# Turning cached keys beside the even layer: each load, turn and store pinned to a projection unit

## The chip, the cores and the metric

The kernel runs on one core of one Trainium2 chip. The metric is the device time of one execution in microseconds (us), as the median over several runs. A core has a matrix engine (TensorE, PE), a vector engine (VectorE, DVE), a scalar engine (ScalarE, ACT), a general engine (GpSimd, POOL), and a queue engine (SyncE, SP) that issues almost all transfers here. Each engine works off its own row of instructions in the order in which they stand; an instruction that waits for something holds everything behind it on its engine.

## What is computed

One inference step of a decoder with two layers and width 1024, on a prompt of 2048 tokens together with 8 sequences that each decode 4 tokens on top of 2048 cached tokens. Layer 0 runs two groups of heads on one input projection: four heads of a gated linear recurrence (HGRN2) and four heads of forgetting attention. Layer 1 is a gated linear attention (GLA). The part that matters here is the forgetting attention of the decoding sequences, whose cached keys and values lie in pages of 128 tokens that a page table names:

```python
def fox_sample(q, k, v, log_f, k_pages, v_pages, logf_pages, page_table):
    ...
    k_past = k_pages[page_table].reshape(db, -1, H, dh)      # 8 sequences x 16 pages x 128 tokens, 4 heads of 128
    v_past = v_pages[page_table].reshape(db, -1, H, dh)
    ...
    logit_past = jnp.einsum('bthd,bshd->bhts', q, k_past) * scale + cum_new[..., None] + suffix_past[:, :, None, :]
    logit_new = jnp.einsum('bthd,bshd->bhts', q, k) * scale + cum_new[..., None] - cum_new[:, :, None, :]
    ...
    p = jax.nn.softmax(jnp.concatenate([logit_past, logit_new], axis=-1), axis=-1)
    return einsum(p[..., :P], v_past) + einsum(p[..., P:], v)

def even_mixer(h, w_in, ...):
    proj = h @ w_in                                          # one projection for both groups of heads
    qa, fa, ia, ga, qb, kb, vb, gb, fb = _split(proj, ...)
    o_a, s_a = gated_linear_chunked(qa, 1 - f, ia, log(f), s0)   # HGRN2
    ...                                                      # forgetting attention, gates, output projection
```

## The kernel before, in words

**Even layer.** `phase_even` (from L1122) works the prompt in two halves of 1024 tokens, and each half is 16 projection units: unit numbers 0 to 15 and 16 to 31. A unit multiplies the half's normalized activations with one block of weights, in a few chunks of columns. `staged` (L1266) runs the units one after another; beside each chunk it issues a step of a later unit's weight preparation (load of the raw weights, row maxima, powers and scales, split into two halves) and calls `beside`. Names of weights tell the unit: `w_Ag`, `w_A10f`/`Aqf`, `w_Bq`, `w_Bk`, `w_Bv`, `w_Cqk`; `pt_...`/`pf_...` are the products in PSUM, `Bk`, `Bv`, `Bg` their evicted results, `Bks`, `Bvs` and `kd`, `vd`, `qd`, `sgd` their split copies and the places in DRAM to which they are stored. `lin_attn` is the recurrence of HGRN2, in `dg`, `gd_A`, `gl_A`, `qA`, `fA`, `o_A`, `py_A`, `y_A`; it runs beside the units, its results go to `yT`. `pow_o` and `kc` are small scale calculations.

**Keys.** The cached keys make 32 tiles, each of four pages of one sequence. A tile `kp` (128 partitions x 4 x 512, 1 MB) comes by four transfers of 256 KB. The page numbers are first loaded to registers of SP (`page_regs`, L1520), and each transfer takes its address from one of them (`page_load`, L1528). For TensorE the keys must lie with the head's dimension on the partitions: DVE turns each of the four pages with one STREAM_TRANSPOSE (`turn_block`, L1532) into a tile `kT`. For the first `PRE` = 16 tiles this is done ahead, in the even layer, by `ahead` (L1534): the turned tile is stored to a place in DRAM (L1548, 1 MB), and the forgetting attention reads it back as `ktd` (L1592). The other 16 are loaded and turned in the forgetting attention itself.

`ahead` is called from `beside`, for chunks 1 and 3 of each unit, with x counting up by two per unit, and starts at x = `PRE0` = 32, the first unit of the second half. Only its page loads are held behind one another:

```python
            with ExitStack() as st:
                if n:
                    st.enter_context(self.tc.issue_after(self.last_page.ins))
                regs = self.page_regs(n % 2, n // 2)
            for x in range(4):
                self.last_page = self.page_load(t, "cache_fox_k", regs[x], x)
```

**What sets the order.** The kernel is written with a scheduling layer. It takes the recorded instructions, models their times, and puts each engine's instructions into a fixed order; work without dependences on its neighbours can come out far from the place in which it was written. `with self.tc.issue_after(x.ins)` pins what is recorded in it to stand behind instruction `x` on its engine's row. Tiles live in rings of buffers by tag: `kp` and `kT` share the ring "wr" with the raw weights (`EWR` buffers); a tile can be written only when the reader of the ring's previous holder is done. Before, the 16 tiles come out back to back: their loads are issued from 352.1 to 583.3 us of the span, their turns stand from 383.2 to 593.8.

**Forgetting attention.** `phase_fox` (from L1350) begins when the last unit's values are there. It interleaves the prompt's attention (scores `s`, DVE's masking and maximum in L1418, `L`, `mx`, `nm`, and the loads of each step: `q`, `k` by a transposing load, `v`, `cb`, `fsg`, L1380 to L1395) with the attention of the decoding sequences: `qs`, `kn`, `sgs`, `vn` (L1604) and `q` (L1617) are its small loads, `qz` its scaled queries (L1625), `sc` its scores against the turned keys (L1692).

Of the kernel before, what the change touches and what calls it, by code (L numbers as in the profile page):

```python
# [8 lines left out]
F32 = mybir.dt.float32  # L9
# [6 lines left out]
ALU = mybir.AluOpType  # L16
# [3 lines left out]
P = 128  # L20
D = 1024
KT = D // P
# [6 lines left out]
NH = 4  # L29
# [10 lines left out]
EWR = 3  # L40
# [10 lines left out]
PRE = 16  # L51
PRE0 = 32
PAST = 3
# [74 lines left out]
class Kern:  # L128
# [200 lines left out]
    def half_unit(self, pool, pps, w, cols, key, nm, undo=None, k=1.0, also=(), raw=("wr", WU), scaler=None, keep=None):  # L329
# [7 lines left out]
        def fetch():  # L337
            t["raw"] = pool.tile([P, KT, raw[1]], F32, tag=raw[0], name=f"wr_{nm}")
            for a, off, n, src in self.sources(w, cols, h):
                with nc.allow_non_contiguous_dma(reason="a few columns"):  # L340
                    nc.sync.dma_start(t["raw"][:, a * h : (a + 1) * h, off : off + n], src)

# [36 lines left out]
    def kept_unit(self, pool, kept, width, nm):  # L379

        t = {}

        def load():
            t["w"] = Parts(self.w_tile(pool, nm, width))
            self.nc.sync.dma_start(t["w"].both.rearrange("p x k c -> p (x k c)"), kept[:, : 2 * KT * width])

        return lambda: None, load, lambda: None, lambda: t["w"]
# [294 lines left out]
    def silu2(self, wp, dst, ps, n, nm, c):  # L682

        nc = self.nc
        th = wp.tile([P, 512], F32, tag="th", name=f"th_{nm}")
        nc.scalar.activation(dst, ps, AF.Copy, scale=c)  # L686
        self.last_th = nc.scalar.activation(th[:, :n], dst, AF.Tanh, scale=0.5)
        self.last_si = nc.vector.scalar_tensor_tensor(dst, th[:, :n], 1.0, dst, ALU.add, ALU.mult)


    def lin_attn(self, wp, pps, hf, h, dv, q, f, k, v, vs, sg, gain, S, s0, s_out, p_out, ydst, nm):
# [26 lines left out]
        def finish(po, g, rows, ncol, cnt):  # L718
# [9 lines left out]
            def out(c0, dcol):  # L728
                for t in range(nt):
                    py = pps.tile([P, 512], F32, tag="gr", name=f"py_{nm}{g}{t}")  # L730
                    for c in range(cnt):
                        nc.tensor.transpose(py[:, c * rows : (c + 1) * rows], on[:rows, c, t * P : (t + 1) * P],
                                            self.ident[:rows, :rows])
                    y = wp.tile([P, 512], F32, tag="y", name=f"y_{nm}{g}{t}")
                    w = TS if g == "S" else cnt * rows

                    for x in range(2 if g == "S" else 1):
                        yo, src, gate = y[:, :w], py[:, :w], sg[t][:, c0 : c0 + w]
                        if g == "S":
# [3 lines left out]
                        nc.vector.scalar_tensor_tensor(yo, src, gain[:, t : t + 1], gate, ALU.mult, ALU.mult)  # L743
                    nc.sync.dma_start(ydst[t][:, dcol : dcol + w], y[:, :w])

            return out

        def levels(ws):
            for w in ws:
# [186 lines left out]
    def even_half(self, hf, act, wpool, wp, pps, npool, S):  # L936
# [54 lines left out]
        def mk_qf(h):  # L991
            def run(W):
                nm = f"A{hf}{h}"
                if h not in self.scales2:
# [6 lines left out]
                                        ALU.mult, ALU.add)  # L1001
                nc.vector.tensor_scalar(f[h][:, :n], f[h][:, :n], self.fb[:, h : h + 1], self.fa[:, h : h + 1],
                                        ALU.mult, ALU.add)
# [5 lines left out]
        def store_cols(dst, t, c0, m):  # L1009

            for a, cnt, dc in self.pieces(hf):
                lo, hi = max(a, c0), min(a + cnt, c0 + m)
                if lo < hi:
                    nc.sync.dma_start(dst[:, dc + lo - a : dc + hi - a], t[:, lo - c0 : hi - c0])

        def mk_bq(hp, which):
            def run(W):
                if which == "q" and hf == 0:
                    self.fox_scale("q", hp)
                for j in range(2):  # L1020
                    h = 2 * hp + j

                    def ev(ps, c0, m, h=h):
                        t = wp.tile([P, 512], F32, tag="c2", name=f"B{which}{hf}{h}{c0}")
                        if which == "q":
                            up, few = self.fsc["q", hp][0], max(0, c0 + m - HALF)
                            u = t.bitcast(F16).rearrange("p (x t) -> p x t", x=2)[:, :, : m - few]
                            nc.scalar.activation(u[:, 0], ps[:, : m - few], AF.Copy, scale=up)
                            nc.vector.scalar_tensor_tensor(u[:, 1], ps[:, : m - few], up, u[:, 0], ALU.mult,
                                                           ALU.subtract)  # L1030
                            dc = hf * HALF + c0
                            nc.sync.dma_start(self.qd[h][:, :, dc : dc + m - few], u)
                            if few:
# [11 lines left out]
        def mk_bkv(hp, which):  # L1045
# [3 lines left out]
            def run(W):  # L1049
# [5 lines left out]
                def ev(ps, g, cnt, m):  # L1055
# [12 lines left out]
                    if m == P:  # L1068
                        u = held[1]
                        for j in range(cnt):  # L1070
                            src = ps[:, j, :256].rearrange("p (h d) -> p h d", h=2)
                            hi, lo = (u[:, g % 2 + j, :, x] for x in range(2))
                            nc.scalar.activation(hi, src, AF.Copy, scale=self.cu[which, hp])
                            nc.vector.scalar_tensor_tensor(lo, src, self.cu[which, hp], hi, ALU.mult, ALU.subtract)
                    if m < P:
# [4 lines left out]
                    elif (g + cnt) % 2 == 0:  # L1080
                        if which == "v":
# [5 lines left out]
                        dst = {"k": self.kd, "v": self.vd}[which][hf][g0 * P : (g0 + 2) * P, 2 * hp : 2 * hp + 2]  # L1087
                        self.last_row = nc.sync.dma_start(dst.rearrange("(g s) h x d -> s g (h x d)", s=P),
                                                          u.rearrange("p g h x d -> p g (h x d)"))
# [32 lines left out]
    def phase_even(self):  # L1122
# [4 lines left out]
        with pool("act", side="right") as ap, pool("w", side="right") as w0, pool("wl", side="right") as wp1, \  # L1127
                pool("wk") as wp0, pool("nrm") as n0, pool("stt") as sp, pool("ps", space=PSUM) as pp0:
            wpool = Pool(w0, {"w": 3, "wr": EWR, "rm": 2, "pow": 2, "lr": 2})
            wp = Pool(wp0, {"c4": 7, "sam": 1, "v4": 3, "sg": 3, "pd": 1, "kt": 2, "y": EY, "xpad": 1, "vs": 3,  # L1130
# [15 lines left out]
            def beside(x):  # L1146
                self.ahead(wpool, x)
                x -= 33
# [101 lines left out]
            drain(last)  # L1250
            self.ahead(wpool, 64)

# [13 lines left out]
    def staged(self, us, a, b, beside=None):  # L1266
# [15 lines left out]
        for j in range(a, b):  # L1282
# [250 lines left out]

    def ahead(self, pool, y):  # L1534


        y -= PRE0
        if y % 2:
            if y // 2 < PRE and y > 0:
                t, tag = self.key  # L1540
                self.key = pool.tile([P, NH * 4, P], F32, tag=tag, name=f"kT{y // 2}"), y // 2
                for x in range(4):
                    self.turn_block(self.key[0], t, x)
            return
        n = y // 2
        if 0 < n <= PRE:
            kt, m = self.key
            self.nc.sync.dma_start(self.kT[m], kt.rearrange("p a s -> p (a s)"))  # L1548
        if 0 <= n < PRE:
            tag = "lr" if y + PRE0 < 32 else "wr"  # L1550
            t = pool.tile([P, 4, 512], F32, tag=tag, name=f"kp{n}")
            with ExitStack() as st:
                if n:
                    st.enter_context(self.tc.issue_after(self.last_page.ins))
                regs = self.page_regs(n % 2, n // 2)
            for x in range(4):
                self.last_page = self.page_load(t, "cache_fox_k", regs[x], x)
            self.key = t, tag

# [724 lines left out]
```

## Time and profile before

| | |
|---|---|
| median of three runs | 2336.53 us (2333.63, 2340.0, 2336.53) |
| the profiled execution's own time | 2332.04 us |
| its span in the trace | 2330.4 us |
| mean granted TensorE clock | 0.987 |
| PE busy | 2203.2 us, 95% of the span |
| DVE busy | 1399.7 us, 60% |
| ACT / POOL busy | 992.1 us, 43% / 731.2 us, 31% |
| transfers | 395.48 MB, 170 GB/s on the mean |

The shares are over the whole span. A share of 95 for PE leaves 127 us of idle time, and in which stretches that lies is read from sums by stretch. The second half of the even layer runs from about 480 to 893 us of the span, the start of the forgetting attention follows. In the rows of the timeline a bracket at the end gives how long the engine sat idle ahead of this instruction, and what released it.

### The profile page before, as it was taken

What the parts mean: (1) busy time and instruction counts of PE and PEld (TensorE: products, weight loads), DVE (VectorE), ACT (ScalarE), POOL (GpSimd) and SP (SyncE); (2) the same over time, 40 slices, a digit from 0 to 9 for tenths busy, and PEclk for the clock granted to TensorE, in tenths of its full rate; (3) what the DMA queues carried; (4) which work ended last, traced back from release to release, by engine and by line L of the source; (5) the groups of instructions that cost most, each with busy time, mean ns of one, the idle gap of its engine ahead of it and who ended that gap; (6) DMA issues with size and microseconds to landing.
All of it is one profiled execution on the core that took longest, in us unless ns stands there. A gap on an engine that the chain in (4) does not pass through costs nothing.

```text
span 2330.4 us, 58046 instructions
## 1 busy us (share of the span) xinstructions
PE 2203.2 (95%) x23316; PEld 1572.3 (67%) x23316; DVE 1399.7 (60%) x3138; ACT 992.1 (43%) x2200; POOL 731.2 (31%) x788
## 2 busy tenths in 40 slices
PE   7999999897999998887998999999999999999998
PEld 5677677763565685554445888777677666666887
DVE  7756568635555456697677545366664655547554
ACT  6434354220221223444566543546544535545343
POOL 2223434000111113423345445144551432322232
PEclk9999999998999999999999999999999999999999
DMA  7343447999642239799884968523233531115554
GB/s 238 120 126 104 147 128 228 321 248 290 202 150 92 95 116 299 252 221 254 283 259 147 338 189 253 147 84 128 76 105 90 128 99 58 47 58 164 165 184 158
DMA packets 364144, 395.48 MB, mean 170 GB/s; under 512 B 108401, under 2 KB 303282, under 8 KB 355682
## 3 DMA queue, kind: packets, MB, share of 16 engines
q1 hardware_dynamic: 361730, 385.15, 55.0%
q0 software_dynamic: 2144, 6.62, 0.8%
q8 instruction: 183, 3.00, 0.5%
q14 instruction: 87, 0.71, 0.1%
HBM read 261.58 MB, written 113.20 MB: 161 GB/s over the span
## 4 chain that ended last, share of the span: by engine, by line
PE 43%; DVE 5%; DMA 5%; issue 2%; ACT 2%; POOL 2%; SPq 1%; POOLq 0%; DVEq 0%; ACTq 0%
PE pt_o L629 4%; PE pt_o L630 4%; PE pt_o L631 4%; PE pt_Cv L629 2%; PE pt_Cv L631 2%; PE pt_Cv L630 2%; DMA pgcache_fox_k<-in_cache_fox_k 2%; PE pt L1454 1%; PE o_C L913 1%; PE pv L1772 1%; DVE L L1418 1%; PE gl_C L760 1%; PE fo L629 1%; PE fo L630 1%; DVE kts L1532 1%
## 5 line engine op out<-in xcount | busy, mean ns | idle before, releaser
L629 PE MATMUL pt_o<-w_o,act 128*128 128x256 f16 x1024 | 278.9, 273 | 0.9 <-ACT sg1C L686 0.9
L630 PE MATMUL pt_o<-w_o,act 128*128 128x256 f16 x1024 | 278.9, 273 | 0.0
L631 PE MATMUL pt_o<-w_o,act 128*128 128x256 f16 x1024 | 278.7, 273 | 0.0
L629 PEld LDWEIGHTS <-act 128*128 128x128 f16 x2304 | 226.7, 98 | 40.1 <-issue 3.3
L630 PEld LDWEIGHTS <-act 128*128 128x128 f16 x2304 | 226.9, 98 | 34.7 <-issue 5.6
L631 PEld LDWEIGHTS <-act 128*128 128x128 f16 x2304 | 226.7, 98 | 30.7 <-issue 1.8
L793 POOL TENSOR_TENSOR kA<-kA,fA 128x512 f32<-128x512 f32 (+1 forms) x56 | 77.0, 1374 | 374.0 <-PE gl_A L760 288.0
L1426 ACT ACTIVATE L<-L,nm,kc 128x512 f32<-128x512 f32 (+3 forms) x160 | 118.2, 740 | 74.6 <-DVE nm L1424 73.1
L1434 POOL TENSOR_SCALAR L<-L,nm 128x512 f32<-128x512 f32 (+3 forms) x160 | 100.7, 644 | 134.7 <-DVE nm L1430 65.5
L629 PE MATMUL pt_Cv<-w_Cv,act 128*128 128x256 f16 (+1 forms) x512 | 141.4, 276 | 1.4 <-DMA act<-xs 1.4
L631 PE MATMUL pt_Cv<-w_Cv,act 128*128 128x256 f16 (+1 forms) x512 | 141.3, 276 | 0.0
L630 PE MATMUL pt_Cv<-w_Cv,act 128*128 128x256 f16 (+1 forms) x512 | 141.2, 276 | 0.0
L1461 ACT ACTIVATE th<-pt 128x512 f16<-128x512 f32 (+3 forms) x159 | 81.6, 528 | 101.2 <-PE pt L1454 97.3
L793 POOL TENSOR_TENSOR kC<-kC,fC 128x512 f32<-128x512 f32 (+1 forms) x56 | 81.2, 1450 | 138.0 <-PE gl_C L760 91.8
L1462 DVE TENSOR_TENSOR tl<-pt,th 128x512 f16<-128x512 f32 (+3 forms) x159 | 94.1, 605 | 12.9 <-ACT th L1461 11.3
L1454 PE MATMUL pt<-ident,L 128*128 128x128 f32 x544 | 90.4, 281 | 7.7 <-DVE tl L1462 4.0
L1454 PEld LDWEIGHTS pt<-ident,L 128*128 128x128 f32 x544 | 65.3, 143 | 36.4 <-DVE tl L1462 10.1
L792 DVE TENSOR_TENSOR qC<-qC,fC 128x512 f32<-128x512 f32 (+1 forms) x56 | 73.3, 1308 | 21.1 <-PE gl_C L760 21.1
L1532 DVE STREAM_TRANSPOSE kT<-kp 128x512 f32<-128x512 f32 x64 | 40.1, 681 | 75.2 <-DMA kp<-in_cache_fox_k 69.5
L1972 ACT ACTIVATE vC<-pt_Cv,kc 128x512 f32<-128x512 f32 (+1 forms) x40 | 24.0, 599 | 134.0 <-PE pt_Cv L631 134.0
L629 PE MATMUL pt_Bv<-w_Bv,act 128*128 128x260 f16 (+1 forms) x256 | 71.5, 279 | 5.6 <-DVE kc L278 3.7
L629 PE MATMUL s<-k,q 128*128 128x512 f16 (+3 forms) x160 | 56.6, 355 | 18.1 <-DVE mx L1418 16.9
(961 smaller groups left out, 6491.3 us busy)
## 6 DMA issues: line engine op xcount, KB each, us to landing
pgcache_fox_v<-in_cache_fox_v SPq DMA_DIRECT2D x128, 256.0 KB, 4.2
kp<-in_cache_fox_k SPq DMA_DIRECT2D x64, 256.0 KB, 6.9
kT<-kT SPq DMA_DIRECT2D x16, 1024.0 KB, 5.7
ktd<-kT SPq DMA_DIRECT2D x16, 1024.0 KB, 9.5
pgcache_fox_k<-in_cache_fox_k SPq DMA_DIRECT2D x64, 256.0 KB, 9.0
yr<-yT SPq DMA_DIRECT2D x16, 1024.0 KB, 7.3
x1d<-xo SPq DMA_DIRECT2D x44, 256.0 KB, 4.3
wr_o<-in_w_out_even SPq DMA_DIRECT2D x32, 256.0 KB, 5.2
```

The lines of the kernel that those rows point to most:

```text
L629: nc.tensor.matmul(ps, lh[0], rh[0], start=first, stop=False)
L630: nc.tensor.matmul(ps, lh[0], rh[1], start=False, stop=False)
L631: return nc.tensor.matmul(ps, lh[1], rh[0], start=False, stop=last)
L792: nc.vector.tensor_tensor(xv[:, :, 1], xv[:, :, 1], t0.to_broadcast([P, nb, w]), ALU.mult)
L793: nc.gpsimd.tensor_tensor(kv[:, :, 0], kv[:, :, 0], t1.to_broadcast([P, nb, w]), ALU.mult)
L1426: self.last_exp = nc.scalar.activation(lt[:, :w], lt[:, :w], AF.Exp, bias=nm[:, 0:1], scale=ib, accum_out=nm[:, 2 + j : 3 + j])
L1434: nc.gpsimd.tensor_scalar(lt[:, :w], lt[:, :w], nm[:, 1:2], 2.0**14, ALU.mult, ALU.mult)
L1454: nc.tensor.transpose(pt[:, w : w + P], rows[b][s // 4][0][:, (s % 4) * P : (s % 4 + 1) * P], self.ident)
L1461: nc.scalar.activation(th[:, a:w], pt[:, a:w], AF.Copy),
L1462: nc.vector.tensor_tensor(tl[:, a:w], pt[:, a:w], th[:, a:w], ALU.subtract)))
L1532: return self.nc.vector.transpose(kt[:, :, 32 * x : 32 * x + 32], t[:, x].rearrange("p (a e) -> p a e", e=32))
L1972: r = nc.scalar.activation(v[h][:, g : g + cnt], ps[:, :, :256], AF.Copy, scale=c)
```

## The change

`PRE0` becomes 16 and now counts units: tile m belongs to unit 16 + m. `staged` calls `ahead` for every chunk n of a unit. In chunk 1 the store of the tile before is recorded, and the page numbers and four page loads of tile m, pinned behind the last marked transfer on SP (`last_sp`). In chunk 3 three of its four turns are recorded, pinned behind the last marked DVE instruction (`last_dve`), and in chunk 0 of the next unit the fourth. Many instructions now set these two markers; their own code is the same. The last tile's end is recorded behind the last unit. The turned tile is named `kt` now. Lines from `staged` on move down by 2 or 3 (L1532 becomes L1534, L1548 becomes L1549, L1592 becomes L1595).

```diff
-PRE0 = 32
+PRE0 = 16
...
-                self.ahead(wpool, x)
...
-            self.ahead(wpool, 64)
+            for n in range(2):
+                self.ahead(wpool, 32, n)
...
-                if beside and n in (1, 3):
-                    beside(2 * j + n // 2)
+                if beside:
+                    self.ahead(self.wpool, j, n)
+                    if n in (1, 3):
+                        beside(2 * j + n // 2)
...
-                    nc.sync.dma_start(ydst[t][:, dcol : dcol + w], y[:, :w])
+                    self.last_sp = nc.sync.dma_start(ydst[t][:, dcol : dcol + w], y[:, :w])
...
-                nc.vector.tensor_tensor(t1, t1, t0, ALU.mult)
+                self.last_dve = nc.vector.tensor_tensor(t1, t1, t0, ALU.mult)
...
+    def ahead(self, pool, u, n):
+        nc, m = self.nc, u - PRE0
+
+        def turns(xs):
+            with self.tc.issue_after(self.last_dve.ins):
+                for x in xs:
+                    self.turn_block(self.kt_ahead, self.kp_ahead, x)
+
+        if n == 0 and 0 < m <= PRE:
+            turns([3])
+        if n == 1 and 0 < m <= PRE:
+            nc.sync.dma_start(self.kT[m - 1], self.kt_ahead.rearrange("p a s -> p (a s)"))
+        if not 0 <= m < PRE:
+            return
+        tag = "lr" if u < 16 else "wr"
+        if n == 1:
+            self.kp_ahead = pool.tile([P, 4, 512], F32, tag=tag, name=f"kp{m}")
+            with self.tc.issue_after(self.last_sp.ins):
+                regs = self.page_regs(m % 2, m // 2)
                 for x in range(4):
+                    self.page_load(self.kp_ahead, "cache_fox_k", regs[x], x)
+        if n == 3:
+            self.kt_ahead = pool.tile([P, NH * 4, P], F32, tag=tag, name=f"kt{m}")
+            turns(range(3))
```

How this moves instructions is seen at three places. The first is DVE's row at the second half's first recurrence; `pow_o` and `kc` are a scale calculation, `rm_Cqk` a weight's row maxima, `dg` and `qA` the recurrence. Before:

```order
L1532 STREAM_TRANSPOSE kT_9872<-kp_9694 128x16x32 x4
L1532 STREAM_TRANSPOSE kT_10287<-kp_10098 128x16x32 x4
L295 TENSOR_REDUCE pow_o_6773<-spr_o_6771 128x1
L306 TENSOR_REDUCE rm_Cqk_7190<-lr_Cqk_6970 128x1 x4
L284 TENSOR_SCALAR pow_o_6773<-pow_o_6773 128x1
L308 TENSOR_REDUCE rm_Cqk_7190<-rm_Cqk_7190 128x1
L285 TENSOR_SCALAR kc<-pow_o_6773 128x1
L286 RECIPROCAL kc<-kc 128x1
L706 COPY_PREDICATED dg<-mdiag,gd_A_6787 128x256
L714 TENSOR_TENSOR qA_6588<-qA_6588,fA_6589 128x1024
L1532 STREAM_TRANSPOSE kT_10498<-kp_10373 128x16x32 x4
L771 COPY_PREDICATED dg<-mlev_820,gl_A_6853 128x128
```

After, the same stretch of DVE's row:

```order
L1534 STREAM_TRANSPOSE kt_6760<-kp_6646 128x16x32 x2
L286 RECIPROCAL kc<-kc 128x1
L1534 STREAM_TRANSPOSE kt_6760<-kp_6646 128x16x32 x2
L295 TENSOR_REDUCE pow_o_6772<-spr_o_6770 128x1
L306 TENSOR_REDUCE rm_Cqk_7189<-lr_Cqk_6970 128x1 x4
L284 TENSOR_SCALAR pow_o_6772<-pow_o_6772 128x1
L308 TENSOR_REDUCE rm_Cqk_7189<-rm_Cqk_7189 128x1
L285 TENSOR_SCALAR kc<-pow_o_6772 128x1
L286 RECIPROCAL kc<-kc 128x1
L706 COPY_PREDICATED dg<-mdiag,gd_A_6786 128x256
L714 TENSOR_TENSOR qA_6587<-qA_6587,fA_6588 128x1024
L771 COPY_PREDICATED dg<-mlev_820,gl_A_6853 128x128
```

Tiles 11, 12 and 13 have gone from here; tile 2 stands ahead of the group, and nothing between `pow_o` and the recurrence.

The second place is SP's row where the even layer ends; `vd` are the last stores of values, the L1389 rows transposing loads of the prompt's keys. Before:

```order
L1088 DMA vd_75<-Bvs_11093 128x2x512
L1088 DMA vd_75<-Bvs_11195 128x2x512
L1604 DMA qs<-qs 128x4x32
L1604 DMA kn<-ks 128x4x32
L1604 DMA sgs<-sgd 128x4x32
L1605 DMA vn<-vs 32x512
L1617 DMA q_11507<-qs 32x16x32 x3
L1088 DMA vd_75<-Bvs_11254 128x2x512
L1387 DMA q_02_11398<-qd 128x2x512
L1389 DMA_TRANSPOSE k_02_11399<-kd_73 128x2x512
```

After, the key tile's loads stand behind the first store, and the sequences' small loads (`qs`, `kn`) behind the third transposing load:

```order
L1530 DMA kp_11103<-in_cache_fox_k 32x4x512
L1088 DMA vd_75<-Bvs_11195 128x2x512
L1088 DMA vd_75<-Bvs_11254 128x2x512
L1389 DMA q_02_11398<-qd 128x2x512
L1391 DMA_TRANSPOSE k_02_11399<-kd_73 128x2x512
L1382 DMA cb_11301<-cbd 128x512
L1549 DMA kT<-kt_11263 128x2048
L1393 DMA v_02_11400<-vd_75 128x4x256
L1397 DMA fsg_11405<-sgd 128x512
L1391 DMA_TRANSPOSE k_03_11593<-kd_73 128x2x512
L1382 DMA cb_11301<-cbd 128x512
L1393 DMA v_03_11594<-vd_75 128x4x256
```

`kp_11103` is tile 15, and the store of L1549 its way out; the loads of `qs` and of `ktd` follow behind `k_10`.

The third place is DVE's row at the same time, where the prompt's first score is read. Before:

```order
L1074 SCALAR_TENSOR_TENSOR Bvs_11254<-pt_Bv_11204,kc,Bvs_11254 128x2x128
L275 TENSOR_REDUCE kc<-vmax 128x1
L1074 SCALAR_TENSOR_TENSOR Bvs_11254<-pt_Bv_11204,kc,Bvs_11254 128x2x128
L1418 ISA L_11313,mx_11308<-s_11309,cm_11306 128x128
L1418 ISA mx_11308 128x1
```

After, the same rows with tile 15 among them:

```order
L1074 SCALAR_TENSOR_TENSOR Bvs_11254<-pt_Bv_11204,kc,Bvs_11254 128x2x128
L275 TENSOR_REDUCE kc<-vmax 128x1
L1074 SCALAR_TENSOR_TENSOR Bvs_11254<-pt_Bv_11204,kc,Bvs_11254 128x2x128
L1534 STREAM_TRANSPOSE kt_11263<-kp_11103 128x16x32 x4
L1420 ISA L_11313,mx_11308<-s_11309,cm_11306 128x128
L1420 ISA mx_11308 128x1
```

All four turns of tile 15 stand ahead of the first score's mask and maximum.

More of the change, by code (lines that the diff above doesn't have):

```diff
@@ L340, in fetch @@
                 with nc.allow_non_contiguous_dma(reason="a few columns"):
-                    nc.sync.dma_start(t["raw"][:, a * h : (a + 1) * h, off : off + n], src)
+                    self.last_sp = nc.sync.dma_start(t["raw"][:, a * h : (a + 1) * h, off : off + n], src)
         def parts():
@@ L384, in load @@
             t["w"] = Parts(self.w_tile(pool, nm, width))
-            self.nc.sync.dma_start(t["w"].both.rearrange("p x k c -> p (x k c)"), kept[:, : 2 * KT * width])
+            self.last_sp = self.nc.sync.dma_start(t["w"].both.rearrange("p x k c -> p (x k c)"), kept[:, : 2 * KT * width])
         return lambda: None, load, lambda: None, lambda: t["w"]
@@ L742, in out @@
                                         for z in (yo, gate))
-                        nc.vector.scalar_tensor_tensor(yo, src, gain[:, t : t + 1], gate, ALU.mult, ALU.mult)
-                    nc.sync.dma_start(ydst[t][:, dcol : dcol + w], y[:, :w])
+                        self.last_dve = nc.vector.scalar_tensor_tensor(yo, src, gain[:, t : t + 1], gate, ALU.mult, ALU.mult)
+                    self.last_sp = nc.sync.dma_start(ydst[t][:, dcol : dcol + w], y[:, :w])
             return out
@@ L1001, in run @@
                                         ALU.mult, ALU.add)
-                nc.vector.tensor_scalar(f[h][:, :n], f[h][:, :n], self.fb[:, h : h + 1], self.fa[:, h : h + 1],
+                self.last_dve = nc.vector.tensor_scalar(f[h][:, :n], f[h][:, :n], self.fb[:, h : h + 1], self.fa[:, h : h + 1],
                                         ALU.mult, ALU.add)
@@ L1013, in store_cols @@
                 if lo < hi:
-                    nc.sync.dma_start(dst[:, dc + lo - a : dc + hi - a], t[:, lo - c0 : hi - c0])
+                    self.last_sp = nc.sync.dma_start(dst[:, dc + lo - a : dc + hi - a], t[:, lo - c0 : hi - c0])
         def mk_bq(hp, which):
@@ L1028, in ev @@
                             nc.scalar.activation(u[:, 0], ps[:, : m - few], AF.Copy, scale=up)
-                            nc.vector.scalar_tensor_tensor(u[:, 1], ps[:, : m - few], up, u[:, 0], ALU.mult,
+                            self.last_dve = nc.vector.scalar_tensor_tensor(u[:, 1], ps[:, : m - few], up, u[:, 0], ALU.mult,
                                                            ALU.subtract)
                             dc = hf * HALF + c0
-                            nc.sync.dma_start(self.qd[h][:, :, dc : dc + m - few], u)
+                            self.last_sp = nc.sync.dma_start(self.qd[h][:, :, dc : dc + m - few], u)
                             if few:
@@ L1073, in ev @@
                             nc.scalar.activation(hi, src, AF.Copy, scale=self.cu[which, hp])
-                            nc.vector.scalar_tensor_tensor(lo, src, self.cu[which, hp], hi, ALU.mult, ALU.subtract)
+                            self.last_dve = nc.vector.scalar_tensor_tensor(lo, src, self.cu[which, hp], hi, ALU.mult, ALU.subtract)
                     if m < P:
@@ L1532, in turn_block @@
         return self.nc.vector.transpose(kt[:, :, 32 * x : 32 * x + 32], t[:, x].rearrange("p (a e) -> p a e", e=32))
[L1534 to L1541, printed above, removed]
-                for x in range(4):
[L1543 to L1558, printed above, removed]
+    def ahead(self, pool, u, n):
[15 more added lines that the diff above has]
+                regs = self.page_regs(m % 2, m // 2)
+                for x in range(4):
+                    self.page_load(self.kp_ahead, "cache_fox_k", regs[x], x)
+        if n == 3:
+            self.kt_ahead = pool.tile([P, NH * 4, P], F32, tag=tag, name=f"kt{m}")
+            turns(range(3))
     def fox_sample(self, fs, pps):
```

6 lines of the change are left out of this document (3 added, 3 removed).

## The prediction

> **What bounds the kernel now.** I read the engines' shares first, then sums by stretch of the span for the part where the moved work stands, then the waits of VectorE (DVE) and of TensorE (PE) there one by one, and last the start of the forgetting attention, where the change puts new work.
>
> The engines' shares, then sums by stretch (stretch, its length, then busy us of PE, its weight loads, DVE, ACT, POOL; granted clock, DMA share, GB/s):
>
> ```profile
> PE 2203.2 (95%) x23316; PEld 1572.3 (67%) x23316; DVE 1399.7 (60%) x3138; ACT 992.1 (43%) x2200; POOL 731.2 (31%) x788
> ```
> ```profile
> 350.00:610.00 260.00, 228.56 (x2293) 157.39 (x2292) 156.82 (x339) 56.61 (x125) 35.24 (x28) 0.95 0.94 270
> 610.00:870.00 260.00, 258.92 (x2933) 177.08 (x2931) 137.78 (x329) 61.88 (x172) 40.48 (x37) 1.00 0.37 119
> 870.00:960.00 90.00, 77.07 (x700) 52.14 (x699) 55.49 (x186) 38.79 (x98) 40.28 (x84) 0.94 0.86 286
> 350.00:440.00 90.00, 82.87 (x1005) 69.07 (x1004) 71.38 (x154) 29.74 (x73) 27.15 (x22) 0.96 0.85 266
> ```
>
> PE bounds the kernel. In 350:610 it idles 260 − 228.56 = 31.4 us at a clock of 0.95, with the DMA at 0.94. In 610:870, work of the same kind, it idles 1.1 us at full clock, and the DMA is at 0.37. All 16 early key tiles are loaded and turned in the first of the two. One row for the turns (busy us, mean ns, then DVE's idle time before them), then their loads:
>
> ```profile
> L1532 DVE STREAM_TRANSPOSE kT<-kp 128x512 f32<-128x512 f32 x64 | 40.1, 681 | 75.2 <-DMA kp<-in_cache_fox_k 69.5 <-DMA kd<-Bks 5.5 <-DMA out_fox_v_p<-Bv 0.2
> ```
> ```profile
> L1528 SPq DMA_DIRECT2D kp<-in_cache_fox_k x64: 316/354/1272, 352.2 to 583.3; - x64
> ...
> DMA to landing us min/median/max: 3.6/6.9/11.9
> ```
>
> DVE stands still 69.5 us for pages, since each turn stands in its row right behind its own load, and what is queued behind the turn stands too. PE's waits in this stretch that name DVE (start, duration, wait and releaser in brackets):
>
> ```profile
> 388.29 0.28 PE L629 MATMUL pt_Bv<-w_Bv,act 128*128 128x260 f16 x1 [1.53 <-DVE Bks L1074]
> 399.54 0.49 PE L913 MATMUL o_A<-S,qA 128*128 128x128 f32 x2 [1.97 <-DVE S L919]
> ...
> 444.89 0.46 PE L277 MATMUL spr_o<-ident,kc 128*128 128x128 f32 x2 [0.79 <-DVE Bks L1074]
> 449.00 0.37 PE L629 MATMUL pt_Bv<-w_Bv,act 128*128 128x256 f16 x1 [3.65 <-DVE kc L278]
> ...
> 511.93 0.38 PE L629 MATMUL pf_Ag<-act,w_Ag 128*128 128x512 f16 x1 [2.34 <-DVE pow_o L295]
> ...
> 524.54 0.38 PE L629 MATMUL pf_A10f<-act,w_Aqf 128*128 128x512 f16 x1 [1.87 <-DVE pow_o L295]
> ...
> 562.70 1.05 PE L760 MATMUL gl_A<-qA,kA 128*32 128x16 f32 x64 [10.76 <-DVE qA L714]
> ...
> 581.86 0.72 PE L760 MATMUL gl_A<-qA,kA 128*32 128x16 f32 x64 [1.40 <-DVE qA L792]
> ...
> 595.19 0.38 PE L629 MATMUL pf_Bq<-act,w_Bq 128*128 128x512 f16 x1 [2.15 <-DVE Bq L1029]
> ```
>
> The longest, 10.76 us for qA, can be followed on DVE itself:
>
> ```profile
> 546.47 2.49 DVE L1532 STREAM_TRANSPOSE kT<-kp 128x512 f32<-128x512 f32 x4 [6.86 <-DMA kp<-in_cache_fox_k]
> 555.70 2.49 DVE L1532 STREAM_TRANSPOSE kT<-kp 128x512 f32<-128x512 f32 x4 [6.74 <-DMA kp<-in_cache_fox_k]
> ...
> 561.42 1.22 DVE L714 TENSOR_TENSOR qA<-qA,fA 128x1024 f32<-128x1024 f32 x1
> ```
>
> qA of the second half's first recurrence stands behind two groups of turns that waited 6.86 and 6.74 us for their pages; PE stood until qA ended at 562.64. The clock went too (window, busy us of PE, clock, DMA share, GB/s):
>
> ```profile
> 400.00:404.00 4.00, 4.00 (x25) 0.62 0.68 251
> ...
> 448.00:452.00 4.00, 3.00 (x15) 0.59 1.05 360
> ...
> 556.00:560.00 4.00, 0.00 (x0) 0.50 0.80 332
> 560.00:564.00 4.00, 1.30 (x65) 0.50 1.00 265
> 564.00:568.00 4.00, 4.00 (x12) 0.50 1.06 208
> ...
> 596.00:600.00 4.00, 4.00 (x74) 0.63 0.76 280
> ```
>
> **The change part by part,** against the profiled execution's own 2332.0 us.
>
> *Stalls that go.* Tile m is now loaded and turned beside unit 16+m, so from about 490 us on, and no turn stands ahead of qA any more. From 500 us on the waits sum to 2.34+1.87+10.76+1.40+2.15 = 18.5. The pair at 444.89 and 449.00 (4.4) stands where DVE waited for pages and goes too. The pair at 388.29 and 399.54 (3.5) lies in 350:440, where DVE was busy 71.38 of 90 us, so I count half, 1.8. Sum 24.7: **−25**. Least: 18.5. Most: all idle time above that of the stretch that follows, 31.4 − 1.1 = 30.3. What is late next at 562 is PE's own weight of projection work, as in 610:870.
>
> *Clock.* Busy time times missing clock: 448:452 3.00×0.41 = 1.2; 560:564 1.30×0.50 = 0.65; 564:568 4×0.50 = 2.0; 596:600 4×0.37 = 1.5; half of 400:404 4×0.38 = 1.5. Sum 6.1: **−6**; ends 0 and 0.05×228.56 = 11.4. The row at 556:560, with PE idle since 552, shows 0.50, and 0.50 stands until 568. [...]
>
> *Turns in the second half.* 64 turns × 0.681 = 43.6 us of DVE's row, 2.7 per unit, now stand beside units 16 to 31. There DVE was busy 137.78 of 260 us, and PE hardly ever waited for it, so most turns fall into gaps of DVE. The cover is narrowest where load and turn stand closest, at tile 11: its first three loads stand behind a gate store of L1014, its fourth behind the yT store, its turns right behind qA. SP and DVE there, and SP's row for the page numbers:
>
> ```profile
> 790.20 1.88 SPq L1014 DMA_DIRECT2D sgd<-Bg  x3
> ...
> 794.52 0.32 SPq L744 DMA_DIRECT2D yT<-y_A  x1
> ```
> ```profile
> 795.52 1.22 DVE L714 TENSOR_TENSOR qA<-qA,fA 128x1024 f32<-128x1024 f32 x1
> 799.48 0.45 DVE L771 COPY_PREDICATED dg<-mlev,gl_A 128x128 f32<-128x128 int8 x1 [2.74 <-PE gl_A L760]
> ```
> ```profile
> L1520 SPq TENSOR_LOAD <-scTs x64: 858/874/3200, 38.3 to 1225.9; - x64
> ```
>
> Page numbers (0.87 us) and issues bring the first three pages to a landing at about 793 + 6.9 = 800, while qA ends at 796.74 and the next DVE work waits until 799.48 anyway: so its three turns (2.0 us) start about then and make the next DVE work some 2.5 us late; with the landing between its ends, 1 to 4 us at tile 11. Tiles 2 and 13 stand next closest, about a median landing apart: 1 us each. The other tiles of the middle have more between load and turn: nothing, hidden by DVE's gaps; if that cover is gone, 2.7 us each. SP issues as many transfers per tile as before, now each behind a store or weight load of the same unit, and 1 MB in and 1 MB out move to where the DMA was at 0.37. Each store waits on SP for its tile's last turn, one chunk earlier; behind it stand the next unit's weight loads, which PE wants a unit later, so a turn late by 2.7 us costs nothing there. **+4** in all. Least 0; most 16×2.7/3 = 15, a third of all turns on PE's path. I take the low part, as the row of 610:870 shows DVE at 53%.
>
> *The start of the forgetting attention.* Three things now stand there that stood at about 590 before: tile 15's load (page numbers and four pages of 256 KB behind a store of vd), its four turns right ahead of DVE's first score of the prompt's attention, and the stores of tiles 14 and 15, in all 3 MB. SP, DVE and PE there, and the turned keys' way back:
>
> ```profile
> 884.07 5.57 SPq L1088 DMA_DIRECT2D vd<-Bvs  x2
> 889.69 1.28 SPq L1604 DMA_DIRECT2D qs<-qs  x1
> ...
> 909.64 6.28 SPq L1389 DMA_TRANSPOSE k<-kd  x1
> ```
> ```profile
> 894.41 0.28 DVE L1418 CUSTOM_DVE_ANT_0 L<-s,cm 128x128 f32<-128x128 f32 x1
> ```
> ```profile
> 907.36 0.41 PE L1692 MATMUL sc<-ktd,qz 128*32 128x128 f32 x4
> ...
> 916.76 1.93 PE L1692 MATMUL sc<-ktd,qz 128*32 128x128 f32 x32 [5.46 <-DMA ktd<-kT]
> ```
> ```profile
> DMA to landing us min/median/max: 5.2/9.5/16.3
> ```
>
> Tile 15's pages are issued from about 885 (first store of vd) + 0.9 to about 888 and land, with the longest landing of 11.9 (the DMA is at 0.86 here), at 894 to 900; with 2.7 us of turns the first score comes at 897 to 903 in place of 894.41: 3 to 9 us late. Behind the turns waits SP: the store of tile 15, and behind it in SP's row the second and third keys of the prompt (two transposing loads of 6.28 us each) and only then qs, which stood at 889.69, and the turned keys' loads. qs is issued at about 903 + 2×6.3 + 2 = 917, the first ktd lands at about 919 + 9.5 = 928, where PE wanted it at 907.36. But PE gets the prompt's scores of these key blocks earlier to fill in, and the 5.46 us wait for ktd falls inside the lag. So between 5 better (only that wait goes) and 21 + 9 = 30 worse; I take **+12**, the first score's delay of 9 and a little for the samples' lag, since the row of 870:960 has 13 us of PE idle already in which part of the lag can lie. [...]
>
> Sum: −25 − 6 + 4 + 12 = −15, so 2317 for the profiled execution. The median of the runs shown, 2336.5, stands 4.5 above it: 2321.5, told as **2321 us**.
>
> **The rivals.**
> *A, the turns only change places (slower).* Each group of turns passes whole to PE: −31 + 43.6 + 12 = +25, 2361 us. It ends slower from the point where 19 of the 43.6 us (44%) pass. For it: in 350:440 the turns stood in a DVE that was busy 71.38 of 90, and PE lost 7.1. Against it: 610:870 has a DVE with 122 us free and a PE that never waited.
> *B, the gain is given back at the forgetting attention.* The samples' lag of 30 us passes whole: −31 + 4 + 30 = +3, 2339 us. For it: ktd's wait of 5.46 us before shows that PE has nothing to put in there. Against it: the prompt's loads come earlier.
> *C, that start costs nothing.* −31 + 4 + 0 = −27, 2309 us, and 2304 if the waits at 388 and 399 and their clock go whole. For it: PE idles there 13 us anyway.
> *D, only the stalls from 500 us on go.* −18.5 − 4.1 + 4 + 12 = −7, 2330 us. For it: the earlier waits stand in a busy DVE, and the turns named none of them. That the change does not do what it says is out: the order holds the turns.
>
> **How the numbers follow.** Chances: forecast 0.55 (alone 2311 to 2330), A 0.08, B 0.12, C 0.15, D 0.10. Some 7 us, 0.3%, is about what a measurement can tell from no change. Faster than 2329.5: the forecast, C and little else, 0.72. Within: B and D and the forecast's edge, less where B runs over 2343.5: 0.18. Slower: A and B's upper end, 0.10. Range 2304 (C with the whole early waits) to 2339 (B), which leaves out A and what lies beyond B and C.
>
> **What would show it.** Right: no wait of DVE for kp in 500:600, PE's waits of 500 us on gone or under 1 us, PE idle under 6 us in 350:610, the clock there at 0.98 or above. Middle: in 610:870 PE idle of 3 to 8 us, with the longest wait behind tile 11's turns. Start of the forgetting attention: DVE's first score 3 to 9 us late against the last Bvs, a PE wait that names ktd or qz. Wrong: PE idle over 20 us in 610:870 (A), or PE idle over 40 in the 90 us from the last projection on (B).

## The result, and the profile after

| | before | after |
|---|---|---|
| median | 2336.41 us (16 runs, 2329.84 to 2345.18) | 2322.49 us (16 runs, 2312.37 to 2330.01) |
| ratio, 95% interval | | 0.9937 [0.9922, 0.9951] |
| profiled execution (its span) | 2332.04 us (2330.4) | 2322.63 us (2320.9) |

The change makes the kernel 0.6% faster, some 14 us where 15.5 were forecast. The stretches after, with the columns of the prediction:

```profile
350.00:610.00 260.00, 253.65 (x2568) 175.78 (x2566) 153.93 (x343) 68.19 (x159) 41.47 (x33) 0.99 0.69 199
610.00:870.00 260.00, 250.88 (x2872) 177.15 (x2870) 151.14 (x343) 56.37 (x151) 39.11 (x39) 0.99 0.65 196
870.00:960.00 90.00, 68.11 (x799) 43.41 (x800) 59.69 (x223) 43.43 (x110) 40.84 (x86) 0.89 0.96 307
```

PE's idle time is 6.4 us in the first stretch (31.4 before) and 9.1 in the second (1.1 before); the DMA's load is even over both, 0.69 and 0.65. The waits of PE that are left or new, the last three at the start of the forgetting attention:

```profile
593.09 0.49 PE L913 MATMUL o_A<-Sx,qA 128*128 128x128 f32 x2 [1.55 <-DVE Sx L919]
...
757.15 0.38 PE L629 MATMUL pf_Bg<-act,w_Bg 128*128 128x512 f16 x1 [1.37 <-ACT Bg L686]
776.75 0.74 PE L760 MATMUL gl_A<-qA,kA 128*32 128x16 f32 x64 [3.74 <-DVE qA L792]
817.68 1.13 PE L900 MATMUL st_A<-v,kts_A 128*128 128x128 f32 x8 [3.10 <-DVE lf L1059]
876.28 0.39 PE L629 MATMUL s<-k,q 128*128 128x256 f16 x1 [6.40 <-DVE Bvs L1074]
881.22 0.48 PE L629 MATMUL s<-k,q 128*128 128x384 f16 x1 [4.12 <-DVE mx L1420]
889.64 0.58 PE L629 MATMUL s<-k,q 128*128 128x512 f16 x1 [6.00 <-DVE nm L1434]
```

The 10.76 us wait for qA and its neighbours from 500 us on are gone. The 1.55 us wait that is left there stands behind turns too, those of tile 4, which waited for no page. On DVE:

```profile
590.92 1.89 DVE L1534 STREAM_TRANSPOSE kt<-kp 128x512 f32<-128x512 f32 x3
592.73 0.30 DVE L919 SCALAR_TENSOR_TENSOR Sx<-S,fA,st_A 128x128 f32<-128x128 f32 x1
```

The turns of tiles 11, 13 and 15 still wait for their pages, right ahead of what PE wants:

```profile
773.86 1.90 DVE L1534 STREAM_TRANSPOSE kt<-kp 128x512 f32<-128x512 f32 x3 [7.74 <-DMA kp<-in_cache_fox_k]
...
815.41 1.90 DVE L1534 STREAM_TRANSPOSE kt<-kp 128x512 f32<-128x512 f32 x3 [5.26 <-DMA kp<-in_cache_fox_k]
...
878.49 2.49 DVE L1534 STREAM_TRANSPOSE kt<-kp 128x512 f32<-128x512 f32 x4 [2.26 <-DMA kp<-in_cache_fox_k]
889.13 0.35 DVE L1420 CUSTOM_DVE_ANT_0 L<-s,cm,mx 128x128 f32<-128x128 f32 x1 [6.33 <-POOL cm L1403]
```

The last row names POOL. What POOL waited for, and what ACT waited for ahead of the 6.40 us wait:

```profile
887.00 0.72 POOL L1622 MEMSET q<- 32x64 f32 x4 [15.47 <-DMA kT<-kt]
```
```profile
874.21 0.47 ACT L1073 ACTIVATE Bvs<-pt_Bv,kc 128x256 f16<-128x256 f32 x1 [7.33 <-DMA vd<-Bvs]
```

POOL's fill of a small query mask uses memory that tile 15's turned keys had until their store landed; the masks `cm` of the prompt's scores stand behind it on POOL. ACT's eviction of values waited for a buffer that a store of `vd` had not left yet.

How far after is ahead of before, at four of PE's instructions (us of the span):

| | before | after | ahead by |
|---|---|---|---|
| first score of the prompt's attention (`s`) | 891.4 | 869.6 | 21.8 |
| last score against the turned keys from DRAM (`ktd`) | 980.3 | 963.7 | 16.6 |
| first product of the output projection (`pt_o`) | 1281.0 | 1266.4 | 14.6 |
| last product of the kernel (`pt_o`) | 2321.3 | 2312.1 | 9.2 |

So the even layer won 22 us, the forgetting attention gave back 7. The 5 us lost behind the first `pt_o` lie in layer 1, whose code is the same: it took 1045.7 us there, 1040.3 before, and 1037.5 to 1044.3 in the ten kernels below, so it differs by several us from one profiled execution to the next. Why is open. The medians are 13.9 apart, close to the 14.6 at the first `pt_o`.

### The profile page after: what moved, and what is told of

It is laid out like the page before. It is cut to its first block, busy times and chain, and to the rows that moved or that the text cites. A ratio compares the mean times of both kernels' runs of the same rounds, so it can differ in the third digit from the quotient of the medians.

```text
span 2320.9 us, 58051 instructions
## 1 busy us (share of the span) xinstructions
PE 2200.1 (95%) x23316; PEld 1571.6 (68%) x23316; DVE 1404.6 (61%) x3138; ACT 991.7 (43%) x2200; POOL 727.8 (31%) x788
## 4 chain that ended last, share of the span: by engine, by line
PE 58%; DMA 8%; DVE 6%; SPq 4%; issue 3%; ACT 2%; POOL 2%; POOLq 0%; DVEq 0%; ACTq 0%
PE pt_o L629 4%; PE pt_o L630 4%; PE pt_o L631 4%; DMA pgcache_fox_k<-in_cache_fox_k 2%; PE pt_Cv L629 2%; PE pt_Cv L631 2%; PE pt_Cv L630 2%; PE pt L1456 2%; PE pv L1775 1%; PE o_C L913 1%; SPq L1522 1%; DMA kp<-in_cache_fox_k 1%; PE gl_C L760 1%; DMA ktd<-kT 1%; PE fo L629 1%
## 5 line engine op out<-in xcount | busy, mean ns | idle before, releaser
L792 DVE TENSOR_TENSOR qA<-qA,fA 128x512 f32<-128x512 f32 (+1 forms) x56 | 67.6, 1207 | 10.8 <-PE gl_A L760 10.8
L629 PE MATMUL pt_Bk<-w_Bk,act 128*128 128x256 f16 x256 | 70.6, 276 | 1.9 <-DVE Bvs L1074 1.9
## 6 DMA issues: line engine op xcount, KB each, us to landing
ktd<-kT SPq DMA_DIRECT2D x16, 1024.0 KB, 11.4
```

The source lines that it names most:

```text
L629: nc.tensor.matmul(ps, lh[0], rh[0], start=first, stop=False)
L792: nc.vector.tensor_tensor(xv[:, :, 1], xv[:, :, 1], t0.to_broadcast([P, nb, w]), ALU.mult)
```

## The experiments

Ratios are to the kernel before, from runs on the same chip in the same series.

**One unit early.** Every tile beside units 15 to 30.

```diff
-PRE0 = 16
+PRE0 = 15
```

> The changed kernel with every tile one unit earlier (units 15 to 30 in place of 16 to 31). Theory: the changed kernel loses about 16 us of PE waits at the start of the forgetting attention (6.40 for Bvs, 4.12 for the maximum, 6.00 for nm), all three hung on tile 15's load, turns and store. With tile 15 gone from there they fall to about the 2.7 us of the kernel before: 8 to 14 us faster than the changed kernel, ratio to before about 0.988. Rival: what is won there is lost again to the wait for the turned keys' loads (5.46 us in the kernel before) or to another wait: ratio as for the changed kernel, 0.994.

Measured: 2311.3 us, 0.9911 [0.9890, 0.9932]. Its waits at the start of the forgetting attention:

```profile
878.02 0.39 PE L629 MATMUL s<-k,q 128*128 128x256 f16 x1 [7.15 <-DVE Bvs L1074]
900.02 1.93 PE L1695 MATMUL sc<-ktd,qz 128*32 128x128 f32 x32 [4.22 <-DMA ktd<-kT]
```

The waits for the maximum and for nm went with tile 15, as the theory had it. The one for Bvs stayed, and 4.22 us for the turned keys came, as the rival had it; a new wait of 3.27 us for a row maximum stands at 490 us, behind turns that waited 20.8 us for their page. So the two waits hung on tile 15, and about half of their 10.1 us was won: by the ratios some 6 us, with intervals that overlap those of the changed kernel. (Tile 0 now stands in the first half and takes its buffers from the ring "lr" in place of "wr".)

**A buffer of its own for the query mask.**

```diff
...
-        bm = q4[:, 512:576].rearrange("p (g c) -> p g c", g=2)
+        bm = self.fx_small.tile([P, 64], F32, tag="bm", name="bm").rearrange("p (g c) -> p g c", g=2)
```

> The changed kernel with one edit: the small query mask that POOL fills (64 columns) gets a buffer of its own in place of memory that tile 15's turned keys had. Theory: POOL's fill waited 15.5 us for the store of tile 15, the prompt's masks (cm) stood behind it on POOL, and PE's 6.00 us wait for nm came from that; it goes, and 3 to 6 us are won against the changed kernel, ratio to before about 0.992. The waits for Bvs (6.4) and for the maximum (4.1) stay. Rival: DVE and SP were late anyway, the wait only gets another name: 0.994.

Measured: 2319.58 us, 0.9945 [0.9928, 0.9963], no different from the changed kernel. PE's waits at that place:

```profile
876.57 0.40 PE L629 MATMUL s<-k,q 128*128 128x256 f16 x1 [5.73 <-DVE Bvs L1074]
882.09 0.48 PE L629 MATMUL s<-k,q 128*128 128x384 f16 x1 [4.70 <-DVE mx L1421]
...
895.75 0.27 PE L630 MATMUL fo<-tl,v 128*128 128x256 f16 x1 [2.45 <-DVE tl L1465]
901.41 1.94 PE L1696 MATMUL sc<-ktd,qz 128*32 128x128 f32 x32 [4.52 <-DMA ktd<-kT]
```

The 6.00 us for nm are gone, so POOL's fill was its cause; 4.52 us for `ktd` and 2.45 for a softmax tile stand in its place. My expectation was wrong: the wait only got another name, since `ktd` was due next and no earlier than in the changed kernel.

**Loads a chunk earlier,** turns as in the changed kernel.

```diff
-        if n == 1:
+        if n == 0:
             self.kp_ahead = pool.tile([P, 4, 512], F32, tag=tag, name=f"kp{m}")
```

> The changed kernel with each tile's loads recorded one chunk earlier (chunk 0 in place of 1), turns as before. Theory: the waits of 3.74 us (qA, behind tile 11's turns) and 3.10 us (lf, behind tile 13's) go with about 1.6 us of clock: 5 to 8 us faster than the changed kernel, ratio to before about 0.991. Rival: other tiles come too close to their buffers' last readers, and new waits of the same size stand elsewhere: 0.994.

Measured: 2311.45 us, 0.9898 [0.9876, 0.9921]: about 9 us better than the changed kernel. The waits of 3.74 and 3.10 us are gone, DVE waits for pages once in the whole even layer (15.9 us for tile 0, beside nothing that PE wants), and the first score comes at 861.3 us in place of 869.6. At the start of the forgetting attention it has 9.52 + 1.76 + 8.13 = 19.4 us of waits for Bvs, maximum and nm, more than the changed kernel's 16.5: the first score came 8.3 us earlier, the store of tile 15 only 6.8 us (874.2 us against 881.0).

**Two units early.** `PRE0 = 14`, units 14 to 29.

> The changed kernel with every tile two units earlier (units 14 to 29). Theory: nothing more is to be won at the start of the forgetting attention than with one unit (the tiles end well ahead of it either way), so within 3 us of the run with one unit earlier. Rival, if store and read-back of the last tiles set that start: several us faster again; or, if the units at the end of the first half have no room in DVE, several us slower.

Measured: 2315.18 us, 0.9921 [0.9903, 0.9940]: 4 us behind one unit early by the medians, which is less than the intervals can tell, and the profiled execution was 1 us shorter (2309.20 us against 2310.47). At the start of the forgetting attention 2.81 us for Bvs and 3.49 for `ktd` are left, but at the end of the first half a tile's pages are late again:

```profile
497.84 0.77 PE L293 MATMUL spr_o<-ident,rm_o 128*128 128x128 f32 x2 [6.02 <-DVE rm_o L308]
```

DVE waited 22.54 us for that page, the one of unit 16. That DVE had no room there, as the rival said, isn't what the trace shows: DVE stood idle. The page's loads went out only at 480.7 us; on SP's row they stand behind transposing loads of the next half's activations (L539), whose last two, from 471.7 us on, took 4.2.

**The kernel before, without turns.** Pages are stored as they came; all transfers stay.

```diff
                 t, tag = self.key
-                self.key = pool.tile([P, NH * 4, P], F32, tag=tag, name=f"kT{y // 2}"), y // 2
-                for x in range(4):
-                    self.turn_block(self.key[0], t, x)
+                self.key = t, y // 2
```

> The kernel before without the 64 turns of the even layer: each page tile is stored to DRAM as it was loaded, so the early keys reach the attention unturned; loads, stores and their bytes stay. Theory (DVE's waits for pages hold up PE): DVE waits for no page any more, PE's idle time in 350:610 falls from 31.4 to some 6 us with the DMA still at 0.9 or more, 25 to 32 us faster than before, ratio about 0.988. Rival (the crowded DMA itself slows this stretch): with the same bytes in the same place PE still idles 20 us or more there, ratio 0.997 or above.

Measured: 2327.25 us, 0.9966 [0.9946, 0.9986]: 10 us won (3 to 13 by the interval), not 25 to 32. The first score of its profiled execution comes only 1.7 us earlier than before (889.7 us against 891.4), so where the rest was won is open. Its stretch, then its waits of PE and of ACT in 350:500:

```profile
350.00:610.00 260.00, 229.05 (x2314) 159.27 (x2312) 126.57 (x280) 57.79 (x128) 37.01 (x30) 0.94 0.95 271
```
```profile
PE pt_Bv L629 <- DVE Bvs L1074: 13.3, 3, 6.9
PE st_A L900 <- ACT kts_A L876: 6.4, 1, 6.4
PE pt_Bk L629 <- DVE Bvs L1074: 6.0, 1, 6.0
```
```profile
ACT Bks L1073 <- DMA out_fox_v_p<-Bv: 11.3, 1, 11.3
ACT Bks L1073 <- DMA kd<-Bks: 8.8, 1, 8.8
```

No turn is left there, DVE waits for no page, the pages are through by 553 us, and PE still idles 31 us, now all of it before 490. Evictions wait for buffers that stores have not left. From issue to landing the stores of `kd` and `vd` in 350:500 take, in the kernel before, in the changed one and in this one:

```profile
DMA to landing us min/median/max: 2.3/4.7/10.0
```
```profile
DMA to landing us min/median/max: 2.2/2.5/6.0
```
```profile
DMA to landing us min/median/max: 2.6/5.7/10.6
```

The stores of the values to their output, for one of which ACT waited 11.3 us, took 3.7 us on the median before, 3.4 in the changed kernel and 8.1 here. So the rival was right for 350:500: the crowd of page transfers holds up PE by itself, through the stores of values and keys. The crowd is also denser than before: without turns the loads end at 541 us in place of 583, and the DMA's share in 350:500 is 1.00 in place of 0.93. (Part of it may be SP's row, whose key stores waited 6.7 us for their pages in 350:500; the two were not separated.)

**The changed kernel, without turns.** Tiles are stored as loaded.

```diff
         def turns(xs):
+            return
...
-            nc.sync.dma_start(self.kT[m - 1], self.kt_ahead.rearrange("p a s -> p (a s)"))
+            nc.sync.dma_start(self.kT[m - 1], self.kp_ahead.rearrange("p a s -> p (a s)"))
```

> The changed kernel without the 64 turns of the even layer (tiles stored as loaded, keys unturned; loads and stores as before). Theory: of the turns in the second half only those at tiles 11, 13 and 15 cost PE anything (waits of 3.74, 3.10 and 4.12 us in the changed kernel), so 7 to 12 us faster than the changed kernel, ratio to before about 0.990. Rival A of the prediction (turn time passes to PE): 20 us or more faster than the changed kernel, ratio 0.985 or below.

Measured: 2311.94 us, 0.9897 [0.9871, 0.9922]: the time that the theory gave, so all 64 turns cost about 9 us. The waits behind the turns of tiles 4, 11 and 13 are gone, though one of 2.26 us for `Sx` stands at 817.05. Those of tile 15 are not, though the theory counted 4.12 us there. PE's waits at the start of the forgetting attention:

```profile
870.51 0.48 PE L629 MATMUL s<-k,q 128*128 128x384 f16 x1 [5.68 <-DVE mx L1420]
...
880.80 0.47 PE L1456 MATMUL pt<-ident,L 128*128 128x128 f32 x1 [7.87 <-POOL L L1436]
```

POOL's fill waits here too, 10.63 us for tile 15's store, so what costs there is mostly the tile's transfers, not its turns. Moving the loads a chunk earlier, with all turns in place, was worth as much by the median, and its first score comes at 861.3 us, here at 864.2; so what turns cost in the middle is mostly a late page. Tile 4's turns show that a turn on time can cost as well, 1.55 us. Beside the run before, this one also shows the crowd alone: the same bytes without turns, spread over 478 to 867 us in place of 353 to 541, leave PE 5.7 us of idle time in 350:610.

**Loads pinned alone.** The changed kernel with the turns' pin taken off. (Stores have no pin, in the changed kernel either.)

```diff
-            with self.tc.issue_after(self.last_dve.ins):
-                for x in xs:
-                    self.turn_block(self.kt_ahead, self.kp_ahead, x)
+            for x in xs:
+                self.turn_block(self.kt_ahead, self.kp_ahead, x)
```

> The changed kernel with the loads pinned and the turns' pin taken off. Theory: a turn can't stand far ahead of its pinned load, so the place of the loads does the work and the result is that of the changed kernel within 5 us, ratio 0.992 to 0.996. Rival: the turns float to right behind their loads, and DVE waits for pages again in most units: ratio 0.998 or above.

Measured: 2337.57 us, 1.0009 [0.9993, 1.0025]: the rival. DVE's wait for pages over the span, and three of PE's waits:

```profile
DVE kt L1534 <- DMA kp<-in_cache_fox_k: 105.6, 16, 15.8
```
```profile
617.12 0.86 PE L760 MATMUL gl_A<-qA,kA 128*32 128x16 f32 x64 [4.05 <-DVE qA L714]
...
803.09 0.65 PE L760 MATMUL gl_A<-qA,kA 128*32 128x32 f32 x32 [3.82 <-DVE fA L794]
...
894.54 0.48 PE L629 MATMUL s<-k,q 128*128 128x384 f16 x1 [12.59 <-DVE mx L1420]
```

The loads are spread, and PE idles 8 us in 350:610; but each of the 16 tiles' turns stands right behind its load, and DVE waits 105.6 us. What the spread won, these waits took.

**Turns pinned alone.** The changed kernel with the loads' pin taken off; the page numbers stand behind the loads of the tile before, as in the kernel before.

```diff
-            with self.tc.issue_after(self.last_sp.ins):
-                regs = self.page_regs(m % 2, m // 2)
-                for x in range(4):
-                    self.page_load(self.kp_ahead, "cache_fox_k", regs[x], x)
+            with ExitStack() as st:
+                if m:
+                    st.enter_context(self.tc.issue_after(self.last_page.ins))
+                regs = self.page_regs(m % 2, m // 2)
+            for x in range(4):
+                self.last_page = self.page_load(self.kp_ahead, "cache_fox_k", regs[x], x)
```

> The changed kernel with the turns pinned and the loads' pin taken off (page numbers stand behind the loads of the tile before). Theory: the turns' place in DVE's row does the work; the loads may go out as soon as their ring has a buffer, so the waits of 3.74 and 3.10 us behind tiles 11 and 13 go too: ratio 0.988 to 0.993. Rival: without their pin the loads run in a crowd again and hold up other transfers: 0.996 or above.

Measured: 2309.51 us, 0.9891 [0.9872, 0.9910]. Its page loads:

```profile
L1530 SPq DMA_DIRECT2D kp<-in_cache_fox_k x64: 316/347/1092, 352.9 to 843.2; - x64
...
DMA to landing us min/median/max: 3.3/7.2/11.8
```

DVE waits for no page in the even layer. The loads don't crowd, they stand spread over 490 us. That the ring spaces them, whose buffers come free only as the pinned turns go on, is likely and was not tested by itself. A landing is slower than in the changed kernel (7.2 us against 5.4) and nobody waits for it.

**Turns pinned alone, one unit early and two.** The same with `PRE0 = 15` and with `PRE0 = 14`.

> Turns pinned and loads free (as in the run with the turns pinned alone), and every tile one unit earlier. Theory: the waits in the middle are gone already; at the start of the forgetting attention those for nm (7.14) and for the maximum (1.76) go, the one for Bvs (6.10, the late landing of the values' stores among the key tiles' transfers) stays, and a wait of some 4 us for the turned keys comes: 2 to 6 us faster than with the turns pinned alone, ratio to before about 0.987. Rival: nothing won, 0.989 to 0.991.

> The same with every tile two units earlier. Theory: the values' stores have the DMA to themselves, so the wait for Bvs falls from 6 to 3 us, and the 6 us wait for a row maximum behind a page at the start of the half, which the earlier run with two units had, doesn't come, since the loads run ahead: ratio to before about 0.985. Rival: the loads crowd the end of the first half, where the next half's activations are moved, and the result is no better than one unit early: 0.988 to 0.991.

Measured: 2296.2 us, 0.9834 [0.9813, 0.9855], and 2301.1 us, 0.9870 [0.9850, 0.9891]. One unit early won more than I gave it: its profiled execution is 4.9 us ahead of the one with the turns pinned alone at the first score (855.9 us against 860.8) and 7.0 at the first `pt_o`. Its stretch, and its waits of PE at the start of the forgetting attention:

```profile
350.00:610.00 260.00, 257.11 (x2681) 180.45 (x2678) 162.35 (x361) 69.06 (x161) 41.10 (x34) 1.00 0.77 223
```
```profile
859.29 0.28 PE L629 MATMUL s<-k,q 128*128 128x256 f16 x1 [3.08 <-DVE Bvs L1074]
...
883.71 1.93 PE L1697 MATMUL sc<-ktd,qz 128*32 128x128 f32 x32 [5.49 <-DMA ktd<-kT]
```

PE idles 2.9 us in 350:610. The wait for Bvs fell to 3.08 too: the last page load goes out at 801 us, and the last values' stores land after 5.3 us (median), not the 7.1 of the run with the turns pinned alone. Two units early has a wait of 5.19 us for a row maximum at 495 us again, so the page of unit 16 is late there with free loads too; its loads go out at 477.6 us, again behind the next half's activations. That one unit early is better than two is not shown: the intervals touch, and the profiled execution of two units early was 2 us shorter. One unit early is 39 us ahead of before, where the change had 14.

## Why the prediction was right

**Stalls, −25.** PE's idle time in 350:610 fell by 31.4 − 6.4 = 25.1 us: 18.3 of it from 500 us on (110 − 90.14 = 19.9 before, 110 − 108.42 = 1.6 after), 6.8 ahead of that. The size and the split are those of the sum; the cause is half of it. From 500 us on it is as told, DVE behind its pages: without turns PE has no idle time in that stretch. For the part ahead of 500 us the step failed that laid the waits to DVE's waits for pages. Of its 69.5 us DVE waited 2.6 there, and the 3.65 us wait for `kc` at 449.00 stands behind four turns whose page was 0.88 us late and whose work took 2.49. DVE's waits for pages before, in 350:500, then its row:

```profile
DVE kT L1532 <- DMA kp<-in_cache_fox_k: 2.6, 3, 1.2
```
```profile
445.62 2.49 DVE L1532 STREAM_TRANSPOSE kT<-kp 128x512 f32<-128x512 f32 x4 [0.88 <-DMA kp<-in_cache_fox_k]
448.04 0.71 DVE L1067 TENSOR_SCALAR Bk<-pt_Bk,kc 128x512 f32<-128x512 f32 x1
448.67 0.28 DVE L278 TENSOR_REDUCE kc<-spr_o 128x1 f32<-128x128 f32 x1
```

Without turns PE's idle time ahead of 500 us grew from 11.6 to 31 us, in the denser crowd; the crowded transfers made the stores of values and keys late (medians of 4.7 us from issue to landing before and 5.7 without turns, 2.5 in the changed kernel). How the 11.6 us divide between turns and crowd was not separated. The change mended both at once, by spreading the transfers and by moving the turns away from their loads, and either alone won little: 10 us without turns in the crowd, nothing with spread loads and turns right behind them.

**Clock, −6.** 0.05 of 228.56 us was missing before, 0.01 of 253.65 after: 11.4 − 2.5 = 9 us, on rounded clocks, where 6 were told.

**Turns in the second half, +4.** Mis-sized: idle time in 610:870 rose by 8.0 us and the clock there lost some 2. Tile 11 stands where it was foreseen, with 3.74 us (1 to 4 told). Tile 13, priced at 1, took 3.10, and the 1.37 us for ACT's gate at 757 had no term. That most turns cost nothing held: of 15 tiles ahead of the last, three have a wait of PE over 1 us behind their turns (4, 11 and 13). That a turn on time is hidden by DVE's gaps did not hold for tile 4 (1.55 us). Rival A is out by the run of the changed kernel without turns.

**Start of the forgetting attention, +12.** Mis-sized the other way: 7.2 us (21.8 ahead at the first score, 14.6 at the first `pt_o`). DVE's first score came 5 us behind the last Bvs (880.90 against 875.74), as told (3 to 9). PE's three waits sum to 16.5 us, against 2.69 + 5.46 before, but the turned keys were less late than worked out and the prompt's scores filled the lag. Their first product stands 31.9 us behind the first score in place of 16.0, so 16 us late where 21 were told: the two transposing loads ahead of `qs` took 2.5 and 2.1 us, and the prediction had priced both at 6.28, the longest row of its kind. Two of the three waits had no step: the prediction looked at SP's and DVE's rows and not at POOL's, where the fill of a mask waited 15.5 us for tile 15's store, and priced the 3 MB of transfers without asking who waits for the values' stores among them. Rivals B and C were both partly there, and neither whole; D is out, as the waits ahead of 500 us went too.

With the 2.4 us that after was behind when it entered the stretch (first `Bk` product at 352.2 us, 349.8 before), 25 + 9 − 10 − 2.4 gives 21.6, close to the lead of 21.8 at the first score.

The sum came close in part by luck. The clock gave 3 us more than told, the second half took 6 more, and the start of the forgetting attention 5 less, and these offset each other. Of the signs, three were missed narrowly: 6.4 us of idle time in 350:610 (under 6 told), a wait of 1.55 us from 500 us on (under 1), 9.1 us of idle time in 610:870 (3 to 8). The range's lower end of 2304 doesn't follow from its working: the halves left out are 1.8 us of waits and 0.8 of clock, which gives 2307.

## What to carry to other kernels

Where a static order decides, try to pin the consumer and leave the load free behind its ring: here that gave 0.9891, both pinned gave 0.9937, and a pinned load with a free consumer, which is just a wait in another place, 1.0009. Here a crowd of transfers cost through the stores whose buffers the evictions need: those of keys and values landed after 4.7 us (median) in the crowd and 2.5 spread, and before the change ACT waited 5.5 and 3.7 us for their buffers. So look at the landing times of stores that are not yours. At the end of a phase follow every queue, and the memory that the next phase takes over; a wait taken away there shows its worth only if the next one in line is not due at the same time: with the mask's own buffer 6.00 us for nm went, 4.52 us for `ktd` came, and the time stayed.

## What the runs showed of the hardware

The granted clock can fall after a short wait, and not after each. Rows of one us in the changed kernel, around the 1.55 us wait that ended at 593.09, then the stretch of the 3.10 us wait at 817.68:

```profile
593.00:594.00 1.00, 0.91 (x6) 0.97 0.02 5
594.00:595.00 1.00, 1.00 (x6) 0.50 0.00 0
...
596.00:597.00 1.00, 1.00 (x4) 0.50 0.00 0
```
```profile
816.00:820.00 4.00, 2.32 (x21) 1.00 0.00 1
```

The first was followed by some 3.4 us at half the clock (593.9 to 597.4), the second, twice as long, by none: 820:824 shows 1.00 too. The wait of 1.55 us for `Sx` behind tile 4's turns stands, each time as long, in the changed kernel and in the three kernels with the turns pinned and the loads free. With the turns pinned alone it ended at 591.16, and PE slowed in the same way: from 592.74 to 594.87 its products of `pf_Bg` start 0.42 to 0.43 us apart, and 0.21 to 0.22 from 595.21 on. With the turns pinned and every tile one unit early (it ended at 588.32) or two (596.88) they start 0.21 to 0.22 us apart from the first on, and one unit early the rows from 588 to 600 stay at 1.00. So the same wait was followed by the slow clock in two executions and not in two others; what decides it is not shown. By estimate, half of 3.4 us, 1.7, can be part of what parts single traces of these kernels.
